# 8 KB weight pieces for the experts, weight loads ahead of layer 1's rows, the router prepared in two steps

## The chip, the cores and the metric

The kernel runs on one core of a Trainium2 chip. The metric is the device time of one execution in microseconds (us). A core has TensorE (PE, with PEld for its weight loads), VectorE (DVE), ScalarE (ACT), GpSimd (POOL) and SyncE (SP), whose queue issues most transfers; 16 DMA engines move the data. Each engine works through its own instructions in order and waits on semaphores for the others.

## What is computed

Two encoder layers over 1024 tokens of 1024 floats. Each mixes tokens, projects, normalises, and then runs a mixture of 16 experts of which each token takes two:

```python
for i in range(DEPTH):
    mixed = na_mixer(x, ...) if i % 2 == 0 else mlstm_mixer(x, ...)
    x = layer_norm(ALPHA * x + mixed @ w_out[i], ln_g[i, 0], ln_b[i, 0])
    x = layer_norm(ALPHA * x + moe(x, router_w, router_b, exp_w_gate[i], exp_w_up[i], exp_w_down[i]),
                   ln_g[i, 1], ln_b[i, 1])
```

In `moe`, a token's scores against 16 experts are biased, the best of four groups of experts is taken, and its two best experts get the token. An expert computes `(silu(x @ w_gate) * (x @ w_up)) @ w_down` with weights of 1024x512, 1024x512 and 512x1024. The results, weighted, are added at the tokens' rows.

## The kernel before

**Products.** A fp32 product is made of three: both factors are split into a high part that PE takes whole and the rest, and `mm3` (L103 to L107) adds high by high (L105), high by low (L106) and low by high (L107) into one PSUM bank. Which operand stands still is seen in the names: `dense<-w_hi,xah` is weights against x.

**Weights** come through `WeightStream` (L28): SP loads a piece into `w_raw` (L58), ACT casts it to `w_hi` (L77), and DVE, or another engine that is named, subtracts for `w_lo` (L78). An expert has six pieces of 1 MB: gate in two halves of the 1024 rows, up likewise, down in two halves of its 1024 columns (`chunk`, `add_gu`, `add_d`, L2106 to L2119). Row `k*128+p` of a weight lies on partition p, so one partition's share of a piece is four runs of 512 floats, 2 KB each.

**The experts** (`moe`, L2128) run in the order SEQ, those with a second tile of 64 tokens (`xb`) alternating with those that have only the tile of 128 (`xa`). For each expert: the tokens are gathered to rows, PE transposes them 128 columns at a time (L2170 for 128 rows, L2176 for 64) with the data as stationary operand and the identity moving; `gate_up` (L2202) makes gate and up in the four banks called dense; ACT and DVE make h; `hposes` transposes it (L2255, L2262); `down` (L2266) makes the output of the expert before. It uses two banks called rlg: for each half of the columns one bank for the 128 rows, and after that for each half one for the 64 rows, which hold high and low part side by side (L2298, L2299). ACT scales a finished bank into `ya` (L2289); DVE adds and scales the 64-row ones (L2306 to L2308). These reads are put in a list, `late`, and issued by `flush` after the next group of products. GpSimd then adds the rows into DRAM, `accd` (L2291). `ahead` (L2184) loads and splits up to three pieces in advance. ACT therefore has casts of coming weights, casts of transposes and reads of finished banks in one queue.

**The output projection** (`out_proj`) goes by tiles of 128 tokens, each with two column halves (`products(t, 0)` and `products(t, 1)`) of eight steps k. Into the steps of the first half it puts, by the table `mid`, work of the tiles before: `ranks` of tile t-2 at k=1 (L1573, L1574, which need `rt` from the router's selection on DVE, L1559), `turn` of tile t-1 at k=2 and k=4 (transposes L1485 of z, which `sums` writes, L1895 or L1897), `logits` at k=7. The selection on DVE (`route`, L1505 to L1569) takes as many small instructions as there are rows of arithmetic on 16 scores. The last two tiles' ranks stand outside the loop.

**The router's weights** are prepared once in layer 0 (`router_weights`, L1426), between units of dense work: a transpose (L1432), a copy on ACT, products and sums over rows on DVE (L1439, L1440), ones by POOL (L1442), a product with these ones (L1444).

**From layer 0 to layer 1.** `moe_norm` (L2398) loads the eight tiles of `accd` (L2407, six buffers), normalises them (statistics by DVE L2439 to L2443 or ACT L2447 to L2452, L2460 on POOL, L2463 and L2466 on DVE), and `first_chunks` transposes them (L831) and makes layer 1's first products, with weights split at L817 (ACT) and L812 (DVE). The order on each engine is set by a planner, `Plan`, which is given each operation's engine, its cost and its predecessors, and which starts next what can start earliest; `lag` is added for a transfer's landing. Its order on SP is z0, ln_g, z1, ln_b, z2 and so on, with the weights between (L2419 to L2429). The same function makes the last norm with its rows given.

**Ahead of layer 1's output projection** the weights are opened while the mLSTM scan ends (L785 to L794): one piece is split with POOL in DVE's place (L793), then the scan's last step runs (`tl.advance`), with L1315 and L1361 on DVE and L1353 on ACT, whose result ACT casts as `yh` (L1868).

## Time and profile before

| | us |
|---|---|
| Median of 3 runs | 2055.79 (2053.3 to 2058.6) |
| The profiled execution, its time | 2056.02 |
| Its span | 2054.0 |
| PE busy | 1863.0 (91%) |
| DVE busy | 1401.3 (68%) |
| ACT busy | 1080.4 (53%) |
| POOL busy | 457.1 (22%) |

The mean clock granted to PE in the profiled execution is 0.961. The page gives, in 40 slices of 51.35 us, how busy each engine was in tenths. A row of the timeline has the start, the time, engine, line, operation, output and operands, and in brackets the idle time ahead of it and what ended that. A row of groups ends in the number of instructions, their busy time, the mean in ns, and the idle time ahead of them. A row of waits names the waiting instruction, the one waited for, the sum, how often, and the longest.

### The profile page before, as it was taken

Reading aid. Unit: us, or ns where it says so; the run is one execution under the profiler, and the core shown is the slowest. Engines: PE = TensorE matmul, PEld = TensorE weight load, DVE = VectorE, ACT = ScalarE, POOL = GpSimd, SP = SyncE. Lnnn points to the kernel's source line nnn. Section 1 sums busy time; section 2 is a strip of 40 time slices with the busy share of each in tenths; the row PEclk is TensorE's granted clock in tenths of the full one; section 3 lists DMA queues with packets and bytes.
Section 4 is the critical chain, followed back from the end, with each engine's and each line's share of the span. In section 5 each row is a group of like instructions: output and inputs, shape, how many; then the busy total and the mean of one; then the engine's idle time right before and its main releaser. Section 6 shows DMA issues by size and latency. Waiting matters only on the chain. (4 is left out here: it accounts for less than half of the span.)

```text
span 2054.0 us, 27927 instructions
## 1 busy us (share of the span) xinstructions
PE 1863.0 (91%) x9860; PEld 1552.1 (76%) x9860; DVE 1401.3 (68%) x2717; ACT 1080.4 (53%) x1772; POOL 457.1 (22%) x386
## 2 busy tenths in 40 slices
PE   7999999998979999999599899998798799999991
PEld 6788888877757877777398778887687587777771
DVE  5466656677767877777576554269878687777775
ACT  4465555662236666666454555444422465666663
POOL 1132222201221222222210000065422121222211
PEclk9999999999979999999799999999899899999996
DMA  5452321135538899999632222111664789999995
GB/s 186 118 134 61 68 56 39 53 121 169 189 130 293 286 297 306 311 309 305 196 128 70 63 82 75 62 32 49 212 207 150 230 267 291 297 309 306 298 286 185
DMA packets 252978, 371.19 MB, mean 181 GB/s; under 512 B 47820, under 2 KB 120868, under 8 KB 252836
## 3 DMA queue, kind: packets, MB, share of 16 engines
q1 hardware_dynamic: 237460, 320.00, 47.5%
q0 software_dynamic: 15376, 49.38, 9.5%
q8 instruction: 79, 1.29, 0.3%
q14 instruction: 63, 0.52, 0.1%
HBM read 300.43 MB, written 65.76 MB: 178 GB/s over the span
## 5 line engine op out<-in xcount | busy, mean ns | idle before, releaser
L78 DVE TENSOR_TENSOR w_lo<-w_raw,w_hi 128x2048 fp32r<-128x2048 f32 (+1 forms) x222 | 470.4, 2126 | 191.9 <-ACT w_hi L77 188.7
L77 ACT CAST w_hi<-w_raw 128x2048 fp32r<-128x2048 f32 (+1 forms) x224 | 396.9, 1780 | 62.9 <-DMA w_raw<-in_exp_w_gate_dram 47.2
L105 PE MATMUL dense<-xT_h,w_hi 128*128 128x512 f32 (+1 forms) x544 | 226.3, 416 | 0.9 <-ACT xT_h L192 0.9
L107 PE MATMUL dense<-xT_h,w_lo 128*128 128x512 f32 (+1 forms) x544 | 208.4, 383 | 1.7 <-DVE w_lo L78 1.7
L106 PE MATMUL dense<-xT_l,w_hi 128*128 128x512 f32 (+1 forms) x544 | 208.1, 383 | 1.0 <-DVE xT_l L193 1.0
L105 PE MATMUL dense<-w_hi,xah 128*128 128x512 f32 x480 | 195.9, 408 | 0.0
L107 PE MATMUL dense<-w_hi,xal 128*128 128x512 f32 x480 | 188.3, 392 | 0.0
L106 PE MATMUL dense<-w_lo,xah 128*128 128x512 f32 x480 | 187.9, 391 | 0.0
L2291 POOL DMA_INDIRECT accd<-ya,la x30 | 80.2, 2675 | 431.1 <-ACT ya L2289 419.6
L105 PE MATMUL dense<-w_hi,yh 128*128 128x512 f32 x288 | 127.6, 443 | 10.7 <-ACT yh L1868 10.6
L106 PE MATMUL dense<-w_lo,yh 128*128 128x512 f32 x288 | 119.9, 416 | 7.6 <-DVE w_lo L93 7.6
L342 ACT ACTIVATE att_p<-att_p,att_st 128x352 f32<-128x352 f32 (+1 forms) x96 | 57.9, 604 | 128.4 <-DVE att_st L340 126.2
L584 POOL TENSOR_TENSOR bias<-bias_raw,masks 128x352 f32<-128x352 f32 (+1 forms) x96 | 85.2, 893 | 163.6 <-DVE att_st L350 145.9
L107 PEld LDWEIGHTS dense<-xT_h,w_lo 128*128 128x128 f32 x544 | 103.6, 191 | 23.2 <-DVE w_lo L78 2.6
L107 PE MATMUL dense<-w_hi,yl 128*128 128x512 f32 x288 | 120.1, 417 | 0.2 <-DVE yl L1801 0.2
L351 DVE TENSOR_SCALAR att_p<-att_p,att_st 128x256 f32<-128x256 f32 (+2 forms) x160 | 112.4, 702 | 5.7
L106 PEld LDWEIGHTS dense<-xT_l,w_hi 128*128 128x128 f32 x544 | 104.6, 192 | 8.3 <-DVE xT_l L193 1.4
L105 PEld LDWEIGHTS dense<-xT_h,w_hi 128*128 128x128 f32 x544 | 104.4, 192 | 8.2 <-ACT xT_h L192 1.0
L105 PE MATMUL rlg<-w_hi,hah 128*128 128x512 f32 x256 | 103.9, 406 | 2.7 <-ACT hah L192 2.7
L107 PEld LDWEIGHTS dense<-w_hi,xal 128*128 128x128 f32 x480 | 90.1, 188 | 20.2
L107 PE MATMUL rlg<-w_hi,hal 128*128 128x512 f32 x256 | 101.4, 396 | 3.5 <-DVE hal L193 3.5
L2215 PE MATMUL dense<-w_hi,xbc 128*128 128x512 f32 x256 | 100.8, 394 | 3.8 <-DVE xbc L193 3.8
(448 smaller groups left out, 4308.9 us busy)
## 6 DMA issues: line engine op xcount, KB each, us to landing
w_raw<-in_exp_w_gate_dram SPq DMA_DIRECT2D x64, 1024.0 KB
w_raw<-in_exp_w_up_dram SPq DMA_DIRECT2D x64, 1024.0 KB
w_raw<-in_exp_w_down_dram SPq DMA_DIRECT2D x64, 1024.0 KB
w_raw<-in_na_w_in_dram SPq DMA_DIRECT2D x20, 512.0 KB
w_raw<-in_w_out_dram SPq DMA_DIRECT2D x8, 1024.0 KB
x1d<-z SPq DMA_DIRECT2D x16, 512.0 KB
accd<-za SPq DMA_DIRECT2D x16, 512.0 KB
z<-accd SPq DMA_DIRECT2D x16, 512.0 KB
```

What stands on the lines that cost most here:

```text
L77: self.nc.scalar.copy(h[:, :n], t[:, :n])
L78: (eng or self.nc.vector).tensor_tensor(l[:, :n], t[:, :n], h[:, :n].bitcast(F), op=OP.subtract)
L105: nc.tensor.matmul(out, lhsT=a[0], rhs=b[0], start=first, stop=False)
L106: nc.tensor.matmul(out, lhsT=a[0], rhs=b[1], start=False, stop=False)
L107: nc.tensor.matmul(out, lhsT=a[1], rhs=b[0], start=False, stop=last)
L342: nc.scalar.activation(self.p, self.p, AF.Exp, bias=st[:, 0:1], scale=-1.0, accum_out=st[:, 1:2])
L351: nc.vector.tensor_scalar(self.p, self.p, st[:, 2:3], None, op0=OP.mult)
L584: nc.gpsimd.tensor_tensor(b[:, :nr], rev[:, w0:w0 + nr, u0:u0 + 32], nb.masks[:, half * 3 + kind].rearrange("p (a b) -> p a b", b=32)[:, :nr],
L2215: nc.tensor.matmul(pb, lhsT=c[:, kk], rhs=w[0][:, k], start=kk == 0, stop=False)
L2291: nc.gpsimd.indirect_dma_start(out=accd[layer], out_offset=bass.IndirectOffsetOnAxis(ap=la[:, 0:1], axis=0), in_=ya, in_offset=None, compu ...
```

## The change

The change has seven parts.

1. The expert pieces are cut so that consecutive rows lie on one partition (row `p*8+k` of gate and up, `p*4+k` of down), and down is cut by rows, not by columns: a partition's share is one run of 8 KB, in pieces of 1 MB as before.
2. To match, x and h are transposed by every eighth or every fourth column (`every`).
3. `down` goes over the two row halves, with both column halves inside; both rlg banks are held for the 128 rows, and the 64 rows take two dense banks. The reads of all of them are issued after.
4. `router_weights` stops ahead of the ones-matrix product and goes on one round of dense units later.
5. `ranks` go from k=1 to k=6 for all tiles in the loop but the last.
6. The piece ahead of layer 1's output projection is no longer split on POOL at that place.
7. `moe_norm` loads two pieces of weights, ln_g, ln_b, and the other weights ahead of z. An empty operation of the planner with lag 9.0 stands for the time at which the sums are there.

The core of the diff:

```diff
                 if i == 2:
-                    router_weights(nb.pool)
+                    router = router_weights(nb.pool)
+                    next(router)
                 if i == 3:
+                    next(router)
...
             tl.ws.load(3)
-            tl.ws.split(nc.gpsimd)
...
         nc.gpsimd.memset(one, 1.0)
+        yield
         p = bank("att_t", 2)
...
-                mid = {1: [lambda: ranks(t - 2)], 2: [lambda: turn(t - 1, 0)], 4: [lambda: turn(t - 1, 1)],
+                mid = {1 if t == 7 else 6: [lambda: ranks(t - 2)], 2: [lambda: turn(t - 1, 0)], 4: [lambda: turn(t - 1, 1)],
...
-        def chunk(w, i, k0, nk, c0, ncol):
+        def chunk(w, i, k0, nk):
...
-                return v.rearrange("o (k p) c -> p (o k) c", p=128)[:, k0:k0 + nk, c0:c0 + ncol]
+                return v.rearrange("o (p k) c -> p (o k) c", p=128)[:, k0:k0 + nk]
...
-            ws.add(chunk(wd, i, 0, 4, 0, 512), (4, 512))
-            ws.add(chunk(wd, i, 0, 4, 512, 512), (4, 512))
+            ws.add(chunk(wd, i, 0, 2), (2, 1024))
+            ws.add(chunk(wd, i, 2, 2), (2, 1024))
...
+    def every(x, n, k):
+
+        return x.rearrange("t (p k) -> t k p", k=n)[:, k]
...
-                        nc.tensor.transpose(p[:, k * 128:(k + 1) * 128], xa[:, (4 * q + k) * 128:(4 * q + k + 1) * 128], ident)
+                        nc.tensor.transpose(p[:, k * 128:(k + 1) * 128], every(xa, 8, 4 * q + k), ident)
...
-                        nc.tensor.transpose(p[:, k * 64:(k + 1) * 64], xb[:, k * 128:(k + 1) * 128], ident[:64, :64])
+                        nc.tensor.transpose(p[:, k * 64:(k + 1) * 64], every(xb, 8, k), ident[:64, :64])
...
-                        nc.tensor.transpose(p[:, k * 128:(k + 1) * 128], ha[:, k * 128:(k + 1) * 128], ident)
+                        nc.tensor.transpose(p[:, k * 128:(k + 1) * 128], every(ha, 4, k), ident)
...
                     yb = pool.tile([64, D], F, name="yb", tag="yb", bufs=1)
                     t3 = pool.tile([64, 512], F, name="t1", tag="t1", bufs=1)
                 ws2 = []
-                for n in range(2):
+                pa = [bank("rlg", 2), bank("rlg", 2)]
+                for c in range(2):
                     w = ws.next()
                     ws2.append(w)
-                    pa = bank("rlg", 2)
-                    for k in range(4):
-                        mm3(nc, pa, [th[:, k], tl[:, k]], [w[0][:, k], w[1][:, k]], k == 0, k == 3)
-                    if n:
-                        flush()
+                    for k in range(2):
+                        for n in range(2):
+                            mm3(nc, pa[n], [th[:, 2 * c + k], tl[:, 2 * c + k]], [x[:, k, n * 512:n * 512 + 512] for x in w],
+                                c + k == 0, c == 1 and k == 1)
                     ahead()
                     flush()
                     if fill:
                         fill.pop(0)()
 
-                    def evac(n=n, pa=pa):
-                        nc.scalar.mul(ya[:, n * 512:n * 512 + 512], pa, la[:, 1:2].bitcast(F))
-                        if n == 1:
-                            nc.gpsimd.indirect_dma_start(out=accd[layer], out_offset=bass.IndirectOffsetOnAxis(ap=la[:, 0:1], axis=0),
-                                                         in_=ya, in_offset=None, compute_op=OP.add)
-                    late.append(evac)
-                for n in range(2 if hb is not None else 0):
-                    w = ws2[n]
-                    pb = bank("rlg", 2)
-                    for k in range(4):
-                        nc.tensor.matmul(pb, lhsT=tc_[:, k], rhs=w[0][:, k], start=k == 0, stop=False)
-                        nc.tensor.matmul(pb, lhsT=tc_[:, k], rhs=w[1][:, k], start=False, stop=k == 3)
+                def evac(n):
+                    nc.scalar.mul(ya[:, n * 512:n * 512 + 512], pa[n], la[:, 1:2].bitcast(F))
+                    if n == 1:
+                        nc.gpsimd.indirect_dma_start(out=accd[layer], out_offset=bass.IndirectOffsetOnAxis(ap=la[:, 0:1], axis=0),
+                                                     in_=ya, in_offset=None, compute_op=OP.add)
+                late.extend([lambda: evac(0), lambda: evac(1)])
+                if hb is None:
+                    return
+                pb = [bank("dense", 4), bank("dense", 4)]
+                for c in range(2):
+                    w = ws2[c]
+                    for k in range(2):
+                        for n in range(2):
+                            for m in range(2):
+                                nc.tensor.matmul(pb[n], lhsT=tc_[:, 2 * c + k], rhs=w[m][:, k, n * 512:n * 512 + 512],
+                                                 start=c + k + m == 0, stop=c == 1 and k + m == 2)
                     flush()
                     if fill:
                         fill.pop(0)()
 
-                    def evac(n=n, pb=pb):
-                        sl = slice(n * 512, n * 512 + 512)
-                        nc.scalar.copy(t3, pb[64:128])
-                        nc.vector.tensor_add(t3, pb[0:64], t3)
-                        nc.vector.tensor_scalar(yb[:, sl], t3, lb[:, 1:2].bitcast(F), None, op0=OP.mult)
-                        if n == 1:
-                            nc.gpsimd.indirect_dma_start(out=accd[layer], out_offset=bass.IndirectOffsetOnAxis(ap=lb[:, 0:1], axis=0),
-                                                         in_=yb, in_offset=None, compute_op=OP.add)
-                    late.append(evac)
+                def evac_b(n):
+                    sl = slice(n * 512, n * 512 + 512)
+                    nc.scalar.copy(t3, pb[n][64:128])
+                    nc.vector.tensor_add(t3, pb[n][0:64], t3)
+                    nc.vector.tensor_scalar(yb[:, sl], t3, lb[:, 1:2].bitcast(F), None, op0=OP.mult)
+                    if n == 1:
+                        nc.gpsimd.indirect_dma_start(out=accd[layer], out_offset=bass.IndirectOffsetOnAxis(ap=lb[:, 0:1], axis=0),
+                                                     in_=yb, in_offset=None, compute_op=OP.add)
+                late.extend([lambda: evac_b(0), lambda: evac_b(1)])
 
             PRE = 4
             lists[seq[0]] = early.la, early.lb
...
         gb, loads, rops = dict(rows or {}), [], []
 
         def add_load(t):
-            loads.append(plan.op(ends[t - nbuf] if t >= nbuf else [], ("s", 1.5, lambda: load(t)), lag=2.0))
+            loads.append(plan.op(ends[t - nbuf] if t >= nbuf else [sums_there], ("s", 1.5, lambda: load(t)), lag=2.0))
 
         def add_row(key):
             def row():
                 gb[key] = bcast_row(pool, key + "2", I[key][layer, 1], nc.sync)
             if not rows:
                 rops.append(plan.op([], ("s", 1.5, row), lag=2.0))
-        add_load(0)
+
+        for f in extra[:2]:
+            f()
         add_row("ln_g")
-        add_load(1)
         add_row("ln_b")
-        add_load(2)
-        for t in range(3, nbuf):
-            if extra:
-                extra.pop(0)()
+        for f in extra[2:]:
+            f()
+        sums_there = plan.op([], ("d", 0.0, lambda: None), lag=0.0 if rows else 9.0)
+        for t in range(nbuf):
             add_load(t)
-        for f in extra:
-            f()
 
         def tile_ops(t):
             if t >= nbuf:
```

How instructions move shows at three places. On PE, in layer 0's output projection, at the third tile; `rlg<-rt,tri` and `rlg<-rt,onesb` are the ranks, `rtr<-ident,z` the transposes. Before:

```order
L107 MATMUL dense<-w_hi,yl 128x512
L1573 LDWEIGHTS tri
L1573 MATMUL rlg<-rt_5029,tri 128x16
L1574 LDWEIGHTS onesb
L1574 MATMUL rlg<-rt_5029,onesb 128x16
L1485 MATMUL rtr<-ident,z 128x128 x8
L105 MATMUL dense<-w_hi,yh 128x512
L106 MATMUL dense<-w_lo,yh 128x512
L107 MATMUL dense<-w_hi,yl 128x512
```

Now:

```order
L107 MATMUL dense<-w_hi,yl 128x512
L1488 MATMUL rtr<-ident,z 128x128 x8
L105 MATMUL dense<-w_hi,yh 128x512
L106 MATMUL dense<-w_lo,yh 128x512
L107 MATMUL dense<-w_hi,yl 128x512
L1576 LDWEIGHTS tri
L1576 MATMUL rlg<-rt_5029,tri 128x16
L1577 LDWEIGHTS onesb
L1577 MATMUL rlg<-rt_5029,onesb 128x16
```

The ranks stood ahead of the transposes and now stand behind them and one more step of products; in later tiles five steps lie between the two places.

On ACT, at an expert with a second tile; `ya<-rlg` are the reads of the 128 rows' banks, `t<-rlg` or `t<-dense` those of the 64 rows', `w_hi` the casts of weights, `hah` that of h. Before:

```order
L2289 ACTIVATE ya<-rlg,la 128x512
L77 CAST w_hi<-w_raw 128x2048
L2289 ACTIVATE ya<-rlg,la 128x512
L2306 COPY t_7179<-rlg 64x512 x2
L77 CAST w_hi<-w_raw 128x2048
L192 CAST hah<-rtr 128x512
L77 CAST w_hi<-w_raw 128x2048
```

Now:

```order
L77 CAST w_hi<-w_raw 128x2048
L2297 ACTIVATE ya<-rlg,la 128x512 x2
L2318 COPY t_7587<-dense 64x512 x2
L77 CAST w_hi<-w_raw 128x2048
L192 CAST hah<-rtr 128x512
L77 CAST w_hi<-w_raw 128x2048
```

The two reads of `ya` stood on both sides of a cast, the second in the middle of the 64-row products; now both stand together behind it, and the 64 rows are read from dense banks.

On SP, at the start of layer 1; `z<-accd` are the rows with the experts' sums, `w_raw` the weights of layer 1's input projection. Before:

```order
L2407 DMA z_9555<-accd_73 128x1024
L243 DMA ln_g_9557<-in_ln_g_dram 128x1024
L2407 DMA z_9559<-accd_73 128x1024
L243 DMA ln_b_9568<-in_ln_b_dram 128x1024
L2407 DMA z_9572<-accd_73 128x1024
L58 DMA w_raw<-in_ml_w_in_dram 128x8x128
L2407 DMA z_9583<-accd_73 128x1024
L58 DMA w_raw<-in_ml_w_in_dram 128x8x128
L2407 DMA z_9607<-accd_73 128x1024
```

Now:

```order
L58 DMA w_raw<-in_ml_w_in_dram 128x8x128 x2
L243 DMA ln_g_9559<-in_ln_g_dram 128x1024
L243 DMA ln_b_9564<-in_ln_b_dram 128x1024
L58 DMA w_raw<-in_ml_w_in_dram 128x8x128 x2
L2419 DMA z_9575<-accd_73 128x1024
L2419 DMA z_9578<-accd_73 128x1024
L2419 DMA z_9582<-accd_73 128x1024
L2419 DMA z_9592<-accd_73 128x1024
L2419 DMA z_9598<-accd_73 128x1024
```

Four pieces of weights and both rows for the norm now stand ahead of the first z, and six loads of z follow each other.

More of the change, by code (lines that the diff above doesn't have):

```diff
@@ L1449, in router_weights @@
             nc.vector.tensor_tensor(rt.wg[:, i], m[:, i].unsqueeze(1).to_broadcast([128, 8, 16]), rt.wg[:, i], op=OP.subtract)
+        yield
     def zero_rows(scratch, flat):
@@ L2038, in out_proj @@
                 for k in range(4):
-                    nc.tensor.transpose(p[:, k * 128:(k + 1) * 128], x[:, (4 * q + k) * 128:(4 * q + k + 1) * 128], ident)
+                    nc.tensor.transpose(p[:, k * 128:(k + 1) * 128], every(x, 8, 4 * q + k), ident)
                 p = p.rearrange("p (k t) -> p k t", k=4)
@@ L2113, in add_gu @@
             for w in (wg, wu):
-                ws.add(chunk(w, i, 0, 4, 0, 512), (4, 512))
-                ws.add(chunk(w, i, 4, 4, 0, 512), (4, 512))
+                ws.add(chunk(w, i, 0, 4), (4, 512))
+                ws.add(chunk(w, i, 4, 4), (4, 512))
         def add_d(i):
-            ws.add(chunk(wd, i, 0, 4, 0, 512), (4, 512))
-            ws.add(chunk(wd, i, 0, 4, 512, 512), (4, 512))
+            ws.add(chunk(wd, i, 0, 2), (2, 1024))
+            ws.add(chunk(wd, i, 2, 2), (2, 1024))
         for n, i in enumerate(SEQ):
@@ L2175, in rest @@
                     for k in range(8):
-                        nc.tensor.transpose(p[:, k * 64:(k + 1) * 64], xb[:, k * 128:(k + 1) * 128], ident[:64, :64])
+                        nc.tensor.transpose(p[:, k * 64:(k + 1) * 64], every(xb, 8, k), ident[:64, :64])
                     split_from_psum(c[:, :, 0:64], c[:, :, 64:128], p.rearrange("p (k t) -> p k t", k=8))
@@ L2261, in rest @@
                     for k in range(4):
-                        nc.tensor.transpose(p[:, k * 64:(k + 1) * 64], hb[:, k * 128:(k + 1) * 128], ident[:64, :64])
+                        nc.tensor.transpose(p[:, k * 64:(k + 1) * 64], every(hb, 4, k), ident[:64, :64])
                     split_from_psum(tc_[:, :, 0:64], tc_[:, :, 64:128], p[:, :256].rearrange("p (k t) -> p k t", k=4))
```

## The prediction

> **What bounds the kernel now.** I read the page first, then the windows by stage, then the waits of TensorE (PE), and last the timeline at each place that the change touches.
>
> ```profile
> span 2054.0 us, 27927 instructions
> PE 1863.0 (91%) x9860; PEld 1552.1 (76%) x9860; DVE 1401.3 (68%) x2717; ACT 1080.4 (53%) x1772; POOL 457.1 (22%) x386
> PE   7999999998979999999599899998798799999991
> DMA  5452321135538899999632222111664789999995
> ```
>
> PE works 91% of the span, 191 us short of all of it. The slices at 6, 5 or 7 tenths are ramps and changes of stage. The expert stages (slices 12 to 19 and 32 to 39) also load the DMA engines to nine tenths, so both need a closer look.
>
> ```profile
> 200.00:250.00 50.00, 50.00 (x299) 43.73 (x298) 30.71 (x68) 28.21 (x78) 14.02 (x17) 1.00 0.30 53
> 850.00:900.00 50.00, 48.97 (x231) 39.21 (x230) 37.53 (x30) 32.62 (x32) 12.32 (x6) 1.00 0.95 306
> 900.00:950.00 50.00, 49.19 (x232) 39.40 (x231) 37.80 (x30) 32.81 (x32) 10.54 (x5) 1.00 0.93 308
> ```
>
> The columns are window, length, then busy us of PE, PE's weight loads, DVE, ACT, POOL, the granted clock, the DMA share and GB/s. PE has no idle time in layer 0's attention and about 1 us in 50 among the experts, at clock 1.00. So whatever PE is spared there counts in full, and so does whatever it is given. DMA at 0.95 is the next bound, 5% away.
>
> **The change part by part.** I sum against the profiled execution, 2056.0 us (span 2054.0 and 2.0 around it); the median of the runs is 2055.79, the same within 0.02%.
>
> *Router in two steps.* PE runs the ones-matrix product right behind the small transpose and waits for what DVE and POOL make of the latter.
>
> ```profile
> 187.36 0.41 PE L1444 MATMUL att_t<-rred,rtmp 128*128 128x64 f32 x2 [3.88 <-DVE rred L1440]
> ```
>
> In the new order this product comes a unit of dense work later, more than 200 PE rows on; DVE and POOL are long done by then, and PE has work queued behind (50.00 of 50 from 200 us on). The wait goes in full: −4 us. Its bounds are −4 and 0, the latter if the dependent steps stood in someone's way at the new place.
>
> *Ranks later.* Four of PE's waits for the router's chain on DVE lie at places that move:
>
> ```profile
> 484.27 0.18 PE L1573 MATMUL rlg<-rt,tri 128*128 128x16 bf16 x1 [3.72 <-DVE rt L1559]
> 496.93 0.17 PE L1573 MATMUL rlg<-rt,tri 128*128 128x16 bf16 x1 [2.58 <-DVE rt L1559]
> 540.83 0.17 PE L1573 MATMUL rlg<-rt,tri 128*128 128x16 bf16 x1 [2.19 <-DVE rt L1559]
> 1552.25 0.17 PE L1573 MATMUL rlg<-rt,tri 128*128 128x16 bf16 x1 [2.06 <-DVE rt L1559]
> 497.42 0.68 DVE L1895 TENSOR_TENSOR z<-z,dense 128x512 f32<-128x512 f32 x1
> 499.59 0.60 PE L1485 MATMUL rtr<-ident,z 128*128 128x128 f32 x4
> ```
>
> They add up to 10.6 us, but they don't all go. The second group of transposes reads z, which DVE writes right behind the same chain: done at 498.10, 1.17 us after the ranks at 496.93, while PE reaches that group at 499.59, 2.66 us after them. Without the ranks' wait PE gets there as much earlier, until z stops it: 2.66−1.17 = 1.5 us a wait is what can be won, for three of the four. At the first one all eight transposes stand right behind the ranks, and almost nothing is won. Three by 1.5 is 4.5; I take −4. The loop's order on DVE is unchanged, so the other bound is no gain at all, if DVE's chain alone sets the pace, and −6.
>
> *One split less on GpSimd*, ahead of layer 1's output projection:
>
> ```profile
> 1454.16 5.71 DVE L1315 SCALAR_TENSOR_TENSOR hs<-nm,sm,hs 128x192 f32<-128x192 f32 x4
> 1454.51 4.49 POOL L78 TENSOR_TENSOR w_lo<-w_raw,w_hi 128x2048 fp32r<-128x2048 f32 x1 [0.81 <-ACT w_hi L77]
> 1463.76 0.79 PE L105 MATMUL dense<-w_hi,yh 128*128 128x512 f32 x1 [10.63 <-ACT yh L1868]
> 1465.54 2.29 DVE L78 TENSOR_TENSOR w_lo<-w_raw,w_hi 128x2048 fp32r<-128x2048 f32 x1 [0.58 <-ACT w_hi L77]
> ```
>
> While POOL splits for 4.49 us, four DVE instructions take 5.71 us together; the last norm of the scan hangs on them, and then ACT's yh, on which PE waits 10.63 us. Without the split beside them DVE saves about 4.3 of these 5.71, and PE starts earlier by that. The split is then done on DVE for 2.29 us, behind ACT's cast, and the second piece of weights comes later by that. Net 4.3−2.3 = −2 us; bounds −4 (the late split hidden) and +2 (DVE no faster without POOL).
>
> *The down products.* This is the largest term. A 64-row product took its PSUM bank from the same two as the 128-row ones, so it had to wait until ACT had emptied one:
>
> ```profile
> PE rlg L2298 <- ACT ya L2289: 17.6, 22, 4.4
> 868.06 1.91 ACT L77 CAST w_hi<-w_raw 128x2048 fp32r<-128x2048 f32 x1 [2.98 <-DMA w_raw<-in_exp_w_gate_dram]
> 870.82 0.70 ACT L2289 ACTIVATE ya<-rlg,la 128x512 f32<-128x512 f32 x1
> 871.40 1.92 ACT L77 CAST w_hi<-w_raw 128x2048 fp32r<-128x2048 f32 x1
> 871.57 0.50 PE L2298 MATMUL rlg<-w_hi,hbc 128*128 128x512 f32 x1 [0.76 <-ACT ya L2289]
> 873.20 0.70 ACT L2289 ACTIVATE ya<-rlg,la 128x512 f32<-128x512 f32 x1
> ```
>
> ACT empties it late because it works in order and the cast ahead waits for weights from the DMA (2.98 us). In the change the 128-row sums hold the two banks through both pieces and the 64-row sums take theirs from the four "dense" banks, empty since the gate products were read. ACT's reads have until the next expert's down products, an expert's time later. The 17.6 us go; what is late next is a dense bank for the next gate product behind the 64-row sums, read within a few us. I take −16; bounds −17.6 and 0. The matmuls are the same in number and shape. At the end of each layer both reads now come behind one more cast, and the last scatter starts later: one read of 0.70 us, so +0.7 a layer, +1.4.
>
> *8 KB pieces.* A weight chunk is still 1 MB, with a quarter of the packets. PE's waits on weights among the experts are in the term above, so 0 here, bounds −4 and 0; the cover is PE's own work.
>
> *Strided transposes.* Rows of 8 KB put consecutive rows of a weight on one partition, so the transposes of x and h now read every eighth or fourth float.
>
> ```profile
> L2170 PEld LDWEIGHTS rtr<-ident,xa 128*128 128x128 f32 x240 | 29.9, 140 | 7.9
> L2255 PEld LDWEIGHTS rtr<-ident,ha 128*128 128x128 f32 x128 | 15.7, 140 | 5.4 <-DVE ha L2200 1.4
> L2176 PEld LDWEIGHTS rtr<-ident,xb 64*128 64x128 f32 x112 | 8.0, 139 | 5.0 <-issue 4.3 <-DVE xal L193 0.7
> L2170 PE MATMUL rtr<-ident,xa 128*128 128x128 f32 x240 | 35.9, 272 | 0.0
> L1440 DVE TENSOR_REDUCE rred<-rwg 128x16 f32<-128x128 f32 x2 | 0.7, 366 | 0.1
> L1669 DVE TENSOR_REDUCE rf<-rbig 1x16 f32<-1x256 f32 x1 | 0.4, 407 | 0.0
> L1528 DVE TENSOR_REDUCE rt<-rt 128x1 f32<-128x4 f32 x16 | 2.5, 154 | 0.1
> ```
>
> The data is the stationary operand, so the stride falls on weight loads. In the group at 499.59 four transposes take 0.60 us and one alone takes 0.272, so each further one costs 0.328/3 = 109 ns; the first of a group lies beside the product ahead of it. Exposed are three in four of 240+128 and of 16 more for the first expert, 288, and of the 64-row ones (groups of eight and four, 192 in all) about 160. No strided read by PE stands in this trace. The lower bound is 0, as a gain has no source. The upper bound comes from DVE: 4 to 256 adjacent floats cost 154 to 407 ns, so 128 would be 278, and the reduction with a 64-byte step takes 366, 88 ns more. 448 by 88 ns is 39 us, and a doubled 109 ns makes about 49. I take 0: 128 floats in 109 ns are 0.85 ns each, while the windows' 231 instructions in 48.97 us, 0.21 us each and most of 512 columns, take one each 0.41 ns. So the array's reads can go twice as fast as a weight load asks for, and there is room; DVE's price stays as a rival.
>
> *Loads ahead of layer 1's rows.*
>
> ```profile
> 1007.11 0.35 SPq L2407 DMA_DIRECT2D z<-accd  x1
> 1010.62 0.69 DVE L2439 BATCH_NORM_STATS2 ln_st<-z 128x6 f32<-128x512 f32 x1 [11.28 <-DMA z<-accd]
> 1015.70 1.28 DVE L2466 SCALAR_TENSOR_TENSOR z<-z,ln_mv,ln_b 128x1024 f32<-128x1024 f32 x1 [1.98 <-DMA ln_b<-in_ln_b_dram]
> 1021.53 1.22 DVE L812 TENSOR_TENSOR w_lo<-w_raw,w_hi 128x1024 fp32r<-128x1024 f32 x1
> 1024.35 1.21 DVE L812 TENSOR_TENSOR w_lo<-w_raw,w_hi 128x1024 fp32r<-128x1024 f32 x1
> 1028.54 1.22 DVE L812 TENSOR_TENSOR qm<-w_raw,qm 128x1024 fp32r<-128x1024 f32 x1 [0.52 <-ACT qm L817]
> 1031.10 1.94 PE L831 MATMUL xp<-ident,z 128*128 128x128 f32 x8 [7.40 <-DVE z L2466]
> 1032.69 0.56 PE L105 MATMUL dense<-xT_h,w_hi 128*128 128x256 f32 x1
> ```
>
> SP's queue is in order: the weights and rows stand behind the first z, which waits for the last scatter until 1007.11. Ahead of it they load and are split while DVE is idle (11.28 us). DVE's chain from 1010.62 to the third transpose then loses three splits (3.65), the wait for ln_b (1.98) and the half-microsecond waits on ACT's casts (0.52 and others); its order is reshuffled too, tile 2 beside tile 0. Laid out in the new order with these durations, the third z is done at about 1023.4 and the first product starts at about 1025.4 for 1032.69: −7.3 us. Bounds −10 and −4 (z alone still waits for the scatter).
>
> Sum: −4 −4 −2 −16 +1.4 −7.3 = −31.9; 2056.0−31.9 = 2024.1, say **2024**.
>
> **The rivals.** *A, the strided reads cost.* Mechanism: a weight load that takes a new piece of memory for each float. Place: PE's 448 exposed loads, all where PE is the bound. Price 39 to 49 us, so 2024+44 = 2068 (2063 to 2073). It decides from 71 ns a load (31.9 us/448); half the price gives about 2046. For it: DVE's 366 against 278. Against: PE is another reader, at its own pace. [...]
>
> *B, the DMA takes over among the experts.* The cast's wait for gate weights (2.98 us at 868.06) shows them just in time. PE faster by 17.6 us in about 800 needs 2% more from engines at 0.95. If the pieces aren't lighter, PE waits for weights instead, and the 16 us are lost: 2040. For it: 0.95 and the casts' waits. Against: 5% of room, and fewer packets. [...]
>
> *C, more comes of it.* The lighter DMA takes the start-up waits of each expert stage too, the ranks and the split reach their far bounds: −4, −2, −2 and −2.7 at layer 1's start, about 2013.
>
> **How the numbers follow.** Forecast 0.55, A 0.2 (a quarter of it at half price), B 0.17, C 0.08. A measurement of this kernel tells 0.3% from no change, 6 us: 2049.6 to 2062.0 is "same". Forecast, C and nearly all of B lie below, with some of A's half price: faster 0.72. A at full price is slower: 0.18. The rest, 0.10, lies between. The range reaches to C with its bounds, 2008, and over most of A, 2070.
>
> **What would show it.** Right: no PE wait at the ones-matrix product; PE waiting on z instead of the ranks, shorter; no PE wait for ACT in the 64-row products; PE's first product of layer 1 about 18 us after the first load of z instead of 25.6 (1032.69−1007.11); transposes still 109 ns apart and weight loads near 140 ns. Wrong: weight loads of the transposes well over 200 ns (A), or PE waits for weights of about 1 us per pair of experts (B).

## The result and the profile after

The changed kernel takes 2028.91 us (median of 4 runs, 2027.17 to 2029.96) where the kernel before took 2055.57 beside it: a ratio of 0.9862 with a 95% interval of 0.9838 to 0.9887, 26.7 us faster. The forecast was 2024, with a range of 2008 to 2070. The profiled execution took 2027.17 us, its span 2025.0, 29 us shorter than before.

The profile after, first PE and the sum of the DMA packets, then the two windows among the experts:

```profile
PE 1865.1 (92%) x9860; PEld 1566.2 (77%) x9860; DVE 1396.3 (69%) x2718; ACT 1081.0 (53%) x1772; POOL 461.8 (23%) x385
DMA packets 179251, 371.20 MB, mean 183 GB/s; under 512 B 47820, under 2 KB 120868, under 8 KB 154532
850.00:900.00 50.00, 50.00 (x235) 41.09 (x234) 38.37 (x30) 33.46 (x32) 12.97 (x6) 1.00 0.94 310
900.00:950.00 50.00, 50.00 (x236) 41.12 (x235) 38.37 (x32) 32.58 (x32) 8.70 (x4) 1.00 0.91 304
```

In these windows PE has no idle time left. The DMA share fell from 0.95 to 0.94 in the first, where 310 GB/s move for 306, and from 0.93 to 0.91 in the second, with 304 for 308. The packets went from 252978 to 179251. But in these two windows PE finished 235 and 236 matmuls in 50 us, and a version below does 240 in the same time: it is busier, and not all of that is work.

The waits of PE: the longest one is now at layer 1's start, the ranks have two of their six left (those outside the loop), the 64-row products none, and some new ones have come.

```profile
PE xp L832 <- DVE ln_mv L2467: 22.9, 1, 22.9
PE rlg L1576 <- DVE rt L1562: 10.9, 2, 5.9
PE dense L105 <- ACT yh L1871: 6.3, 1, 6.3
PE rtr L1488 <- DVE z L1898: 4.5, 1, 4.5
PE rlg L105 <- ACT ya L2297: 2.5, 2, 1.3
PE dense L106 <- DVE w_lo L78: 2.4, 3, 1.8
PE rtr L1488 <- DVE z L1900: 1.3, 2, 0.7
```

PE runs 9860 matmuls in both kernels, in nearly the same order, so the time between two of them, counted on PE, gives the stages. In us, from the two profiled executions:

| stage | before | after | difference | forecast |
|---|---|---|---|---|
| layer 0's start, not touched | 55.7 | 58.0 | +2.3 | 0 |
| around the router's weights | 26.8 | 23.3 | −3.5 | −4 |
| output projection 1 | 160.5 | 156.4 | −4.1 | } −4 |
| output projection 2, behind its start | 132.9 | 132.7 | −0.2 | } for both |
| start of output projection 2 (split) | 32.2 | 30.9 | −1.3 | −2 |
| experts of layer 0 | 390.6 | 384.9 | −5.7 | } −16 for both, |
| experts of layer 1 | 395.5 | 382.1 | −13.4 | } strides at 0 |
| layer 1's start | 68.7 | 67.6 | −1.1 | −7.3+0.7 |

These make −27.0 of the 29.0 us; the stages between take the rest. By stages the router, the projections and the split came out within 1 us, the experts' sum was off by 3.1 us (−19.1 for −16), and layer 1's start by 5.5. The experiments show that the experts' sum hides larger errors of both signs. The +2.3 of layer 0's start is no effect of the change, as the stage takes 55.9 us in a second profile of the changed kernel (e8_after); this profile has 3.4 us at a granted clock of 0.50 there (half clock, below), from 30.9 us on, where the kernel before has none.

### The profile page after: what moved, and what is told of

It reads as the page before. It is cut to its first block, busy times and chain, and to the rows that moved or that the text cites. A ratio compares the mean times of both kernels' runs of the same rounds, so it can differ in the third digit from the quotient of the medians.

```text
span 2025.0 us, 27944 instructions
## 1 busy us (share of the span) xinstructions
PE 1865.1 (92%) x9860; PEld 1566.2 (77%) x9860; DVE 1396.3 (69%) x2718; ACT 1081.0 (53%) x1772; POOL 461.8 (23%) x385
## 3 DMA queue, kind: packets, MB, share of 16 engines
q8 instruction: 79, 1.29, 0.3%
## 5 line engine op out<-in xcount | busy, mean ns | idle before, releaser
L2299 POOL DMA_INDIRECT accd<-ya,la x30 | 75.0, 2501 | 399.9 <-ACT ya L2297 389.6
L105 PEld LDWEIGHTS dense<-w_hi,xah 128*128 128x128 f32 x480 | 90.7, 189 | 17.3
```

Of the source, the lines that this page charges most:

```text
L105: nc.tensor.matmul(out, lhsT=a[0], rhs=b[0], start=first, stop=False)
L2299: nc.gpsimd.indirect_dma_start(out=accd[layer], out_offset=bass.IndirectOffsetOnAxis(ap=la[:, 0:1], axis=0), in_=ya, in_offset=None, compu ...
```

## The experiments

The kernel before took a median of 2060 to 2062 us on the chips of the experiments, so they are compared by their ratio to it on their own chip, and by stages.

**The bank alone** (e3_banks): the kernel before with one edit.

```diff
                     w = ws2[n]
-                    pb = bank("rlg", 2)
+                    pb = bank("dense", 4)
```

> The kernel before with one edit: the 64-row down products take a dense bank instead of an rlg bank; the pieces, the loops and all else are as before. Theory: the bank alone makes the 17.6 us of PE's waits for ACT's reads, which then go: 2055.6-17 = 2039 us, between 2037 and 2041. Rival: the wait is only the visible end of weights that come late; freed of it, PE waits for w_hi or w_lo by as much, and the time stays above 2050.

Measured: 2037.73 us, ratio 0.9889 (0.9865 to 0.9912), 23 us faster on that chip, for the 17 that were expected. The windows among the experts:

```profile
850.00:900.00 50.00, 50.00 (x239) 40.66 (x238) 39.02 (x32) 33.54 (x32) 12.00 (x6) 1.00 0.99 316
900.00:950.00 50.00, 50.00 (x240) 40.76 (x238) 38.95 (x30) 33.76 (x33) 9.75 (x4) 1.00 0.96 308
L2298 PE MATMUL dense<-w_hi,hbc 128*128 128x512 f32 x128 | 50.5, 394 | 0.0
```

One word makes most of the change's gain. The expert stages shrink from 390.6 and 395.5 us to 382.3 and 382.9, 20.9 in all, with 2 KB pieces, and with DMA at 0.99 no wait for weights takes the place of the old one. That is 3.3 us more than the 17.6 us of the waits' row, since a wait costs more than its idle time. Behind twenty of the 22 waits, as at 871.57, the first product's successor starts 0.34 us later and not 0.23, which makes 2.2 us. The other two are the longest (2.21 and 4.42 us). Behind them PE's granted clock is 0.50 for 3.4 and 6.8 us; the second of these stretches, in the kernel before:

```profile
1731.50:1738.30 6.80, 4.34 (x10) 3.47 (x11) 5.69 (x4) 5.31 (x7) 1.74 (x1) 0.50 0.96 348
```

PE is busy for 4.34 and 3.24 us of the two, at half clock; half of these 7.58 us, up to 3.8 us, is the estimate of what that costs. So the 22 waits cost up to 23.6 us. Against that, PE's other waits in the two stages, for x and h, grow from 10.5 to 13.6 us. The balance is 20.5 of the 20.9 us; other half-clock stretches of these single executions are not in it, so the last 1 or 2 us are not settled.

**The strides** (e1_plain, e2_contig). The first has plain rows, so adjacent columns are transposed and the pieces are 2 KB (down 4 KB) again; the loops of `down` stay as changed. The second keeps the 8 KB pieces and transposes adjacent columns, which pairs columns with rows that don't belong together.

```diff
# both
-        return x.rearrange("t (p k) -> t k p", k=n)[:, k]
+        return x.rearrange("t (k p) -> t k p", k=n)[:, k]
# e1_plain alone
-                return v.rearrange("o (p k) c -> p (o k) c", p=128)[:, k0:k0 + nk]
+                return v.rearrange("o (k p) c -> p (o k) c", p=128)[:, k0:k0 + nk]
```

> The changed kernel with rows k*128+p on partition p again, so that x and h are transposed by adjacent columns, while down stays cut by rows (2 KB runs for gate and up, 4 KB for down). Theory S: the strided weight loads of the 64-row transposes cost 46 to 60 ns each, with the transposes of h in 128 rows about 10.7 us in all, and the size of the pieces carries nothing: in groups the 64-row transposes go back from 111 and 123 ns to 63, and the time is 2029-11 = 2018 us. Rival P: the 8 KB pieces carry a gain by the DMA; without them PE waits for weights among the experts, and the time stays at 2029 or goes over it, up to 2035, although the transposes are faster.

> The changed kernel with its 8 KB pieces, but x and h transposed by adjacent columns, so that products pair columns with rows that don't belong together; the work is the same in number and shape. Theory S: 2018 us, as without the pieces; 64-row transposes at 63 ns. Rival P: pieces and fast transposes together, 2018 us or a little less, and the difference to the kernel with plain rows (up to 17 us) is what the pieces are worth.

Measured: 2020.38 us for plain rows (ratio 0.9813, 0.9784 to 0.9841) and 2021.39 for 8 KB with adjacent columns (0.9809, 0.9785 to 0.9834). A group of each kind from the timeline, the change first and then plain rows:

```profile
760.67 1.09 PE L2184 MATMUL rtr<-ident,xb 64*128 64x64 f32 x8
750.65 0.70 PE L2270 MATMUL rtr<-ident,hb 64*128 64x64 f32 x4
845.09 0.63 PE L2263 MATMUL rtr<-ident,ha 128*128 128x128 f32 x4
708.51 0.60 PE L2178 MATMUL rtr<-ident,xa 128*128 128x128 f32 x4
```

```profile
756.27 0.71 PE L2184 MATMUL rtr<-ident,xb 64*128 64x64 f32 x8
839.47 0.60 PE L2263 MATMUL rtr<-ident,ha 128*128 128x128 f32 x4
703.99 0.60 PE L2178 MATMUL rtr<-ident,xa 128*128 128x128 f32 x4
```

Before, the 64-row group of h took 0.46 us:

```profile
757.74 0.46 PE L2262 MATMUL rtr<-ident,hb 64*128 64x64 f32 x4
```

The groups of 128 rows hardly notice the stride; those of 64 rows do. The weight loads themselves became longer in both, from the 140 and 139 ns that the prediction shows:

```profile
L2178 PEld LDWEIGHTS rtr<-ident,xa 128*128 128x128 f32 x240 | 36.0, 190 | 5.1
L2184 PEld LDWEIGHTS rtr<-ident,xb 64*128 64x128 f32 x112 | 13.4, 200 | 5.0 <-issue 4.3 <-DVE xal L193 0.7
```

Fourteen groups by 0.38, sixteen by 0.24 and 32 by 0.03 us are 5.3+3.8+1.0 = 10.1 us. The two expert stages agree: 767.0 us in the change and 755.1 with 8 KB and adjacent columns, 11.9 less. Plain rows give 759.6. So theory S holds for the stride. For the pieces it holds in the windows, where PE is full either way:

```profile
850.00:900.00 50.00, 50.00 (x240) 40.74 (x239) 38.95 (x30) 33.17 (x33) 12.70 (x6) 1.00 0.95 321
```

```profile
850.00:900.00 50.00, 50.00 (x238) 40.71 (x237) 39.11 (x31) 32.77 (x32) 12.47 (x6) 1.00 0.98 319
```

The first is 8 KB with adjacent columns, the second plain rows: 0.95 against 0.98 of the DMA for nearly the same work (240 and 238 matmuls). What the pieces bring shows at the entry of layer 0's experts, where the first products of h wait for its low part. The rows are the change and plain rows:

```profile
614.99 0.50 PE L107 MATMUL rlg<-w_hi,hal 128*128 128x512 f32 x1 [0.44 <-DVE hal L193]
612.18 0.50 PE L107 MATMUL rlg<-w_hi,hal 128*128 128x512 f32 x1 [1.60 <-DVE hal L193]
```

This wait is 0.15 to 0.44 us in the five kernels with 8 KB (the change, e2_contig and three of those below) and 0.76 to 1.78 us in the eight with 2 KB, the kernel before among them. At the entry of layer 1's experts it is about 1.7 us in the change as well as in plain rows. Over both expert stages all waits of PE (idle times over 0.15 us) make 6.7 to 8.6 us in those five, and 9.0 to 11.3 in the six with plain rows (this one and five below): 2 to 3 us for the pieces. From 765.2 us with the bank alone the two stages go to 759.6 with plain rows, cut by rows, and to 755.1 with 8 KB and adjacent columns. The latter 4.5 us are more than the waits and lie within what varies, as the plain rows' kernels lie between 757.6 and 762.3 us; the medians of the two don't differ. Of the 5.6 us before that, PE's waits have 3.4 (13.6 and 10.2 us); the cut by rows was not tried by itself.

**Which steps cost** (e5_steps): x is transposed by every n-th float, n = 1 to 7 in the seven experts that have a second tile and that `moe` transposes itself, so columns and rows don't belong together here either.

```diff
+    def steps(x, k, i):
+        n = i if i < 8 else i - 7
+        return x[:, k:k + 127 * n + 1:n] if n > 1 else x[:, k * 128:(k + 1) * 128]
```

> The changed kernel in which the transposes of x read every n-th float, with n = 1 to 7 in the experts with a second tile (64-row transposes) and n = 1 to 8 in the others (128-row ones only in part the same), so products pair columns and rows that don't belong together; number and shape of the work are as in the change. The table that comes out is the spacing of transposes in a group by step. [...] Rival any step: every step over 1 costs the same, 110 ns already at n = 2. Rival distance: the cost grows with the step, n = 2 near 63 and n = 7 the slowest.

Measured: 2030.72 us, in a single run. The 64-row groups of layer 0, n = 1 to 7 from top to bottom:

```profile
624.13 0.71 PE L2188 MATMUL rtr<-ident,xb 64*128 64x64 f32 x8
661.02 1.16 PE L2188 MATMUL rtr<-ident,xb 64*128 64x64 f32 x8
710.04 1.12 PE L2188 MATMUL rtr<-ident,xb 64*128 64x64 f32 x8
759.00 1.18 PE L2188 MATMUL rtr<-ident,xb 64*128 64x64 f32 x8
808.07 1.13 PE L2188 MATMUL rtr<-ident,xb 64*128 64x64 f32 x8
857.15 1.29 PE L2188 MATMUL rtr<-ident,xb 64*128 64x64 f32 x8
906.44 1.20 PE L2188 MATMUL rtr<-ident,xb 64*128 64x64 f32 x8
```

Any step over one costs about the same, already n = 2, whose group takes 1.16 us for the 0.71 of n = 1; n = 6 costs somewhat more, 1.29 us. That is the rival "any step". What makes a step slow is not shown. An estimate from the spacings of this case takes that of a group as the larger of two times: the moving of the identity, about 109 ns for 128 columns and 63 for 64, and the load of the data, at most 63 ns for adjacent floats and 110 to 135 ns for others. By it the moving hides most of the slow load in 128 rows (109 to 126 ns apart by step in this run, the 126 at n = 6), and in 64 rows it doesn't; no run times the two by themselves.

**Layer 1's order of loads undone** (e4_norm): the change with `moe_norm`'s old order of z, rows and weights.

```diff
-        for f in extra[:2]:
-            f()
-        add_row("ln_g")
-        add_row("ln_b")
...
+        add_load(0)
+        add_row("ln_g")
+        add_load(1)
+        add_row("ln_b")
```

> The changed kernel with the order of loads in moe_norm as before: z0, ln_g, z1, ln_b, z2 and so on. Theory: the loads ahead of z share the DMA engines with the last scatter and delay it by about 3.8 us (from POOL's issue to z's issue 9.96 us now, 6.13 us before), which takes most of the 4.9 us that the shorter chain from z to the first product gives. Undone, the issue of z comes back to 6.1 us behind the scatter's, the first product to about 25.6 us behind z, and the time is 2029 to 2031 us. Rival: the delay of z has another reason, and the loads ahead are worth the forecast 6.6 us: 2035 us, with z still 10 us behind the scatter.

Measured: 2029.5 us, ratio 0.9849 (0.9819 to 0.988), the same as the change. POOL's scatter, z's issue and the first product, in the change:

```profile
984.58 1.41 SPq L58 DMA_DIRECT2D w_raw<-in_ml_w_in_dram  x2
989.00 1.56 POOL L2299 DMA_INDIRECT accd<-ya,la  x1 [5.16 <-DVE xm L882]
993.44 1.86 SPq L58 DMA_DIRECT2D w_raw<-in_ml_w_in_dram  x2
998.96 2.85 SPq L2419 DMA_DIRECT2D z<-accd  x6
1019.64 0.56 PE L105 MATMUL dense<-xT_h,w_hi 128*128 128x256 f32 x1
985.00:1000.00 15.00, 2.34 (x11) 1.55 (x9) 2.54 (x4) 3.42 (x4) 1.56 (x1) 0.67 1.01 269
```

And with the old order:

```profile
986.87 1.56 POOL L2299 DMA_INDIRECT accd<-ya,la  x1 [5.25 <-DVE xm L881]
993.09 0.34 SPq L2419 DMA_DIRECT2D z<-accd  x1
1018.48 0.56 PE L105 MATMUL dense<-xT_h,w_hi 128*128 128x256 f32 x1
985.00:1000.00 15.00, 0.04 (x1) 0.00 (x0) 3.06 (x8) 1.17 (x3) 3.09 (x2) 0.65 0.63 172
```

With the loads ahead, z to the first product takes 20.68 us instead of 25.39, which is the gain of 4.7; but from the scatter's issue to z's it takes 9.96 us instead of 6.22, which is the loss of 3.7. These differences repeat: z comes 8.9 to 10.0 us behind the scatter in seven executions with the change's order, and 6.1 to 6.4 in three with the old one. In the meantime the DMA engines are full (1.01 against 0.63 in these windows): in the change's window the queue of the loads takes 66.1% of the 16 engines' time and that of the scatters 34.5%. The trace has the scatter's own packets, 0.52 MB: in the change the first starts 5.0 us behind the scatter's issue, for 2.1 with the old order, and they run for 4.6 us, for 3.6. So the theory holds in that the loads delay the scatter, but most of the delay, 2.9 us, is a later start of its packets and 1.0 a slower run.

**Fewer loads ahead** (e6_w, e6_ln, e10_mid), on plain rows. e6_w sends two pieces of weights ahead and ln_g, ln_b and the others behind z0; e6_ln only ln_g and ln_b; e10_mid is e6_w with the third and fourth piece between the z.

```diff
# e6_w; sums_there is the planner's operation for the sums
         for f in extra[:2]:
             f()
...
+        add_load(0)
+        add_row("ln_g", [sums_there])
+        add_load(1)
+        add_row("ln_b", [sums_there])
...
+        for f in extra[2:]:
+            f([sums_there])
```

> The kernel with plain rows (e1_plain) in which only two pieces of weights go ahead of z at the start of layer 1; ln_g, ln_b and the third and fourth piece stand behind z0 and later. Theory contention: what lies ahead of z delays the last scatter by its bytes; 1 MB instead of 3 MB costs about 1.3 us instead of 3.8 us, and ln_b makes z wait up to 2 us as before, so 1 to 2 us faster than with plain rows alone, about 0.9806 of the kernel before. Rival: the delay doesn't go by bytes but is the wait behind any load (3.8 us again), and the time is that with plain rows or 1 us more.

> The kernel with plain rows in which only ln_g and ln_b go ahead of z at the start of layer 1 and all weights stand between the z as before the change. Theory contention: the two rows delay the scatter by about 1.3 us and save the 2 us wait for ln_b, while the splits of weights are back in DVE's chain (+3.7 us): the first product 24 to 25 us behind z and the time equal to plain rows within 1.5 us, rather slower. Rival: the rows alone carry what the loads ahead bring, and it is 2 us faster.

> Plain rows, two pieces of weights ahead of z and the third and fourth between the z, behind the third and the fourth. Theory contention: the scatter is as early as with two pieces ahead (6.7 us from its issue to z's), the first product comes 25 to 26 us behind the last product of the expert instead of 32 to 33, and the third piece no longer holds up the stage behind it: 4 to 6 us faster than plain rows, 15 us faster than the change. Rival: the pieces between the z delay these as before the change, and nothing is won over plain rows.

Measured: e6_w 2017.72 us, ratio 0.9793 (0.9779 to 0.9806); e6_ln 2018.15, 0.9795 (0.978 to 0.981); e10_mid 2021.04, 0.9805 (0.9778 to 0.9832), on a chip where plain rows had 0.981. e6_w's start of layer 1:

```profile
984.51 1.38 SPq L58 DMA_DIRECT2D w_raw<-in_ml_w_in_dram  x2
989.12 1.56 POOL L2299 DMA_INDIRECT accd<-ya,la  x1 [5.29 <-DVE xm L882]
995.81 0.34 SPq L2419 DMA_DIRECT2D z<-accd  x1
1012.25 0.58 PE L105 MATMUL dense<-xT_h,w_hi 128*128 128x256 f32 x1 [0.21 <-ACT xT_h L840]
```

The scatter takes 6.69 us to z's issue, nearly as with nothing ahead, and z takes 16.44 us to the first product, less than in either order: the planner now puts the first products ahead of the third tile's transposes. Some of that is given back behind: the whole of layer 1's start takes 62.9 us, against 68.0 with plain rows. e6_ln has 65.3 and e10_mid 62.7. As times of a stage these are gains of 5.1, 2.7 and 5.3 us, for the 1 to 2, about 0 and 4 to 6 that were expected. The bytes alone don't set the delay: e6_ln also sends 1 MB ahead, and z comes 8.08 us behind the scatter for e6_w's 6.69; what makes the difference is not shown. In the medians they are not safe: the intervals overlap those of plain rows (0.9784 to 0.9841 and 0.9792 to 0.9829). e10_mid was expected 15 us ahead of the change and is 6.9 ahead of it in the medians of their chip.

**Ranks and split undone** (e7_undo), on plain rows: `ranks` at k=1 for all tiles and the split on POOL again, as in the kernel before.

> The kernel with plain rows in which the ranks stand at k=1 again and the one split is on POOL again. Theory: each of three waits at the ranks gives 1.4 us more and the split 1.4 to 2 us, so 5 to 6 us slower than plain rows, about 0.984 of the kernel before; PE's waits at the ranks come back (four of 2 to 4 us), and PE's wait for yh goes from 6.3 to 10.6 us. Rival: what was won at either place is lost by the next wait, and the time is that with plain rows within 2 us.

Measured: 2029.02 us, ratio 0.9854 (0.9839 to 0.987), on the chip of e6_w and e6_ln. Waits of PE, with both undone and then in plain rows:

```profile
PE rlg L1577 <- DVE rt L1563: 19.8, 6, 5.7
PE dense L105 <- ACT yh L1872: 10.6, 1, 10.6
```

```profile
PE rlg L1576 <- DVE rt L1562: 11.5, 2, 5.8
PE dense L105 <- ACT yh L1871: 6.3, 1, 6.3
PE rtr L1488 <- DVE z L1898: 5.8, 2, 4.5
```

The ranks' waits fall by 8.3 us and those for z come to 5.8: the moved step wins what the waits differ by, some 1.5 us each at three places, and loses one at the first. The start of the projection takes 32.4 us with the split on POOL and 31.0 without, 1.4 less, where yh comes 4.3 us earlier and what follows takes 3 us back. The wait for yh is 6.3 us in all ten kernels without that split and 10.6 in all three with it, but the stage takes 29.7 to 33.3 us in the ten and 31.9 to 32.4 in the three, so that the 1.4 us are not safe. For the ranks the waits are clearer than the times: PE's waits in output projection 1 and behind the start of output projection 2 make 30.4 to 32.9 us in the ten kernels with ranks at k=6 and 34.7 to 36.5 in the three at k=1 (before, e3_banks, e7_undo). On its own chip e7_undo's profiled execution is 11.0 us longer than e6_w's, and these two have nearly the same time at half clock in the projections, 53 and 55 us: 4.7 us lie in the order of loads, 5.0 in the projections and 1.1 at the start. So ranks and split together are worth 4 to 6 us, near the theory.

**The change and plain rows side by side** (e8_after, e9_plain), the kernels as they were.

> The changed kernel once more, beside plain rows and the new order on the same chip. Both theories of the strided reads and of the loads expect 0.985 to 0.987 of the kernel before; its stages say how far a stage moves by itself from run to run (the output projections by up to 6 us so far).

> Plain rows once more on the same chip. Theory (strided reads cost 9 to 12 us, pieces of 8 KB carry nothing): 0.995 of the changed kernel, 9 to 12 us faster. Rival (the difference seen so far was one of chips): within 4 us of the changed kernel.

Measured: the change 2027.96 us, ratio 0.9832 (0.9811 to 0.9854); plain rows 2024.6, 0.981 (0.9792 to 0.9829). The expert stages are 766.7 and 762.3 us. Only 3 to 4 us, then, on this chip and in the medians, the range of the rival, and the intervals overlap. The transposes differ by the same 10 us as before (the group times are those shown). In this execution plain rows lose 4.4 us at the end of layer 1's experts: PE waits 1.66 us there for h, whose last step on DVE comes behind a split of weights, and then works for 6.8 us at a clock of 0.50. The other end and e1_plain's two have no such wait.

**What moves by itself.** Output projection 1 took 160.5, 156.8 and 160.8 us in three kernels with ranks at k=1 (before, e3_banks, e7_undo) and 154.3 to 160.6 in ten with ranks at k=6. The trace shows why: PE's granted clock is 0.50 for stretches of 3.4 us or two to four times that. The first row is the kernel before, the second the change:

```profile
565.00:570.00 5.00, 5.00 (x22) 3.78 (x21) 4.72 (x21) 0.00 (x0) 2.71 (x2) 0.50 0.50 161
485.00:495.00 10.00, 10.00 (x34) 8.22 (x34) 7.50 (x36) 1.64 (x4) 1.99 (x2) 0.50 0.12 45
```

In the ten kernels with ranks at k=6 the stage's time goes by the sum of these stretches: 20 us of them in the three that take 154.3 to 154.7 us, 26 to 27 in the five of 156.4 to 157.4, and 38 in the two of 160.4 and 160.6. So 17 us more at half clock make 6 us. Most stretches come with a wait of PE of 2 us or more, but not all: over the whole traces of the kernel before and of the change, 23 of the 31 that start ahead of PE's last product start in such a wait or up to 1.4 us behind it. Behind the wait of 4.5 us for the first z, which all ten have, one follows every time, of 3.4 us in six of them (e4_norm is one: the window from 485 to 495 us has 0.87 and 52 matmuls), of 10.2 in the change and of 13.7 in three. What sets its length is not shown.

## Why the prediction was right, and where it wasn't

The sign, the size to within 5 us and the main mechanism, the bank, were right. That the size came so near is luck, as the terms below show. By its steps:

- *Router*: −3.5 for −4. The product is gone from 187 us, and no wait stands at its new place.
- *Ranks*: −4 was forecast for three times 1.5 us. The three waits, 2.58, 2.19 and 2.06 us, became none (1.3 in plain rows), 0.75 and 0.59, much as worked out from z behind the ranks. At the first tile, where "almost nothing is won", 3.72 and 0.52 us became one of 4.5. PE's waits in the two projections fell by 5.7 us and their time by 4.3.
- *Split*: −1.3 for −2, and as said: yh comes 4.3 us earlier, and 3 us are lost behind it instead of 2.3. The stage varies by as much between alike kernels, so the size is not confirmed.
- *Down products*: the mechanism was right and the term mis-sized. −16 was taken from the 17.6 us of waits, as if something new would appear; it measured −20.9 with the bank alone. What a wait costs behind it was left out: the later second product, 0.11 us behind each of twenty of the 22, and the half clock behind the two longest, for 3.4 and 6.8 us.
- *8 KB pieces*: 0 was taken and −4 the bound, with PE's own work as cover. It covers them inside the stages; at the entry of layer 0's experts PE waits for what comes behind the weights, and over both stages 2 to 3 us of waits went.
- *Strided transposes*: the step that failed is "I take 0: ... the array's reads can go twice as fast as a weight load asks for, and there is room". It took the spacing of 109 ns for the time of a load. By the estimate from the spacings it is the time of moving the identity, and the load's own time was hidden. So it held for 128 rows (0.60 and 0.63 us a group for 0.60) by luck of what lies beside, and not for 64: 10 to 12 us. Rival A named the place, PE's weight loads, and the sign, at a price four times too high (39 to 49 us), because it took the loads of 128 rows for exposed too, and 88 to 109 ns a load where the 64-row ones cost some 50 to 60 more; it stayed under its point of decision. The signs didn't decide it either: the loads take 190 to 211 ns, between the "near 140" that was to show the forecast right and the "well over 200" for A.
- *Loads ahead*: the step that failed is that z "waits for the last scatter until 1007.11" and that the loads ahead of it leave this as it is. The chain behind z became shorter by 4.9 us (25.58 to 20.68) where 7.3 was forecast, and the scatter itself became longer by 3.8 (6.13 to 9.96), so that −1.1 was left of −6.6. The prediction has no term for what the loads do to the scatter, whose packets start 2.9 us later and run 1.0 us longer with the loads ahead.
- *Ends of the layers*: 0.7 us a layer was allowed; PE waits 1.3 us for a bank in the last `down` of each, 2.5 in all, since both rlg banks are held until both reads are done.
- *Rival B* did not come: PE is full at a DMA share of 0.94 in the change and even at 0.99 with 2 KB pieces.

Taken together, the bank gave 4.9 us more than forecast, the cut by rows with its pieces 5.6 to 10 where 0 was put (5 to 7 of it PE's waits), the strides cost 10 to 12 and the loads brought 5.5 less: errors of both signs, and so the total is nearer than its terms.

Plain rows with less ahead of z have the lowest ratios here, 0.9793 (e6_w) and 0.9795 (e6_ln) of the kernel before, for 0.9862 and 0.9832 of the change on its two chips; they are not told apart from each other or from plain rows alone.

## What to carry to other kernels

PE's 17.6 us of waits for PSUM banks that ACT empties in its order went by taking banks that are free anyway, and that was worth 20.9 us: count a wait's idle time plus what follows it, here a second product 0.11 us later and, behind the two longest waits, 3.4 and 6.8 us at half clock. A layout that makes transfers larger can be paid for on the engine that is the bound, here with 10.1 us of PE's for 2 to 3 us of its waits: ask which of two overlapped times an interval shows before saying that the hidden one has room. Loads that are moved ahead of a chain's transfer can hold it up, as z's issue came 9.96 us behind the scatter's here for 6.22, with the DMA engines at 1.01 for 0.63; look at the share of the engines in that stretch, and send ahead only what has landed by then (with two pieces ahead it came 6.69 us behind). Before a difference of stages is put down to an edit, compare the time that each spent at half clock: 17 us more of it made 6 us in output projection 1.

## What the hardware showed that was not expected

- Transposes of 64 rows of fp32 data follow each other every 110 to 124 ns when 128 columns are loaded with any step of 2 to 5 or of 7 or 8 floats, and every 135 at a step of 6, against 63 for adjacent ones; the size of the step hardly matters. Their weight loads take 200 and 211 ns for 139 and 138, and those of 128 rows 190 and 204 for 140, where a group of four takes 0.60 and 0.63 us for 0.60.
- PE's granted clock fell to 0.50 for 3.4 us or a multiple of it, 23 times of 31 in a wait of 2 us or more or up to 1.4 us behind one (the kernel before and the change). Behind the same wait of 4.5 us it stayed there for 3.4 to 13.7 us in ten executions, and it moved the stage of output projection 1 by up to 6 us.
- An indirect scatter of 512 KB held up the load behind it for 8.9 to 10.0 us in seven executions with about 3 MB of loads ahead of that load, and for 6.1 to 6.4 us in three without; in the change its packets started 2.9 us later and ran 1.0 us longer.
